# Transposed storage of the inversion's second operands, and a 32-byte pad ahead of the inner activations

## The chip, the cores and the metric

The kernel runs on one core of a Trainium2 chip. The core has five engines that run their own instruction streams and meet through semaphores: TensorE (matmul; its weight loads are shown apart, as PEld), VectorE (DVE), ScalarE (ACT), GpSimd (POOL) and SyncE (SP), which here issues most DMAs. SBUF holds 128 partitions; matmul results go to PSUM. The metric is device microseconds of one execution of the whole program; lower is better.

## The reference, cut to what matters

A two-layer diffusion backbone over 512 latent tokens and 256 context tokens of width 1024. The first layer mixes tokens by windowed attention and by a bidirectional RWKV-7 scan, the second by a Fourier transform; each layer ends in a dense block with a hidden width of 4096. What the change touches is the scan and the dense block:

```python
def step(S, inp):
    r_t, w_t, k_t, v_t, kk_t, a_t = inp
    s_kk = jnp.einsum('bhvk,bhk->bhv', S, kk_t)
    S = (S * w_t[:, :, None, :]
         - s_kk[..., None] * (kk_t * a_t)[:, :, None, :]
         + v_t[..., None] * k_t[:, :, None, :])
    return S, jnp.einsum('bhvk,bhk->bhv', S, r_t)

def channel_mlp(h, w1, w2):
    return jnp.square(jax.nn.relu(h @ w1)) @ w2
```

Everything is float32.

## The kernel before, in words

**The scan, by chunks.** The scan is computed in chunks of 64 steps, two chunks at a time, in six stages `i` (two of context, four of latent tokens), both directions and eight heads together. Inside a chunk the recurrence is a triangular system, so each stage needs the inverses of 32 unit-triangular 64x64 matrices. `prep(i)` and `chunkmats(i)` make the matrices (tiles `ab`), `inverse(i)` replaces their diagonal blocks by inverses, and `chain_step(i, j)` uses them on TensorE. The six inversions come one after another between about 220 and 550 us, woven with the attention and with the projections.

**`inverse(i)`.** The 32x32 diagonal blocks go out through DRAM (tile `Dg`) and come back into tile `Minv` (`M` and its second half `Mb`) with each of the 64 blocks on two of the 128 partitions, one for each of its 16x16 diagonal blocks. VectorE then inverts the 128 of them at once, every partition its own, by block doubling: `R` (tile `Rt`) holds the inverses of the diagonal blocks of size `m`, and for m = 2, 4, 8 two block products give the off-diagonal blocks of size `m`. A product of two m x m blocks has two instructions: `tensor_tensor` (line 820) forms all m*m*m products into `Mt` (`tt`), with the sum's index innermost, and `tensor_reduce` (line 823) sums the innermost index. Step 0 multiplies a block of `M` by a block of `R` into the small tile `pp`, step 1 a block of `R` by `pp` into `R`. For the last doubling, from 16 to 32, the 16x16 products are split over the two halves of the partitions, eight columns each, and made in two halves of eight rows (`r0`): lines 838 (the wide product, 1024 elements per partition) and 840 (its sum), four of each per inversion. There step 0 multiplies by `Yh` (columns 256 to 384 of `Mb`, filled by two ScalarE copies at lines 830 and 831 from the inverse in `R`), and step 1 by `pp`. Further ScalarE copies (832 to 834) lay out other operands, and 843, 844 and 846 put the result in place; then it goes back through DRAM (`D2`, `D3`), and small matmuls (863 to 872) finish the 64x64 inverses in `ab`.

The second operand of every such product is a matrix of which column `j` is multiplied by row `i` of the first, so the sum's index runs down a column. Stored row by row, as `Yh` and `pp` are, a column is read with a stride of a row: 8 elements at line 838 and 820 with m = 8, 4 with m = 4, 2 with m = 2 (32, 16 and 8 bytes). Where step 0 of line 820 reads its column from `R`, the stride is 32 elements.

**The dense blocks.** `mlp(l, ...)` runs twice. Each float32 matrix is split into a rounded part and the rest (`whi`/`wlo`, `hhi`/`hlo`, `zhi`/`zlo`), and `mm3` makes each product from three matmuls (lines 306, 307, 308): weights 128x128 held in the array, 512 columns of activations streamed past. The weights are loaded by DMA into `st`, rounded by ScalarE (line 294) and subtracted by VectorE (line 295). In each of two halves of the hidden width, 16 blocks first stream the normed input `hhi`/`hlo` (the first three blocks of a layer stream `uhi`/`ulo`) and write the squared ReLU as `zhi`/`zlo` (lines 1466 and 1467); then eight output blocks `m` stream the 16 pairs `zhi`/`zlo`. Those are the inner activations. They and the operands of the Fourier layer are taken with `zq` from pool `Q`, 34 slots of 2048 bytes per partition; `hhi`, `uhi` and the weights come from pools `H` and `wp`. For the very last output block, `last()` runs its 512 columns as two parts of 256.

**Order and addresses.** Each engine runs its instructions in the order in which the scheduler put them, and the same holds for DMA issues on SP. Tile addresses come from the pools, in the order of their first use; a pool's tiles begin behind each other. As built, the start addresses per partition are these:

| tiles | first byte, modulo 2048 | modulo 64 |
|---|---|---|
| `whi`, `wlo`, `hhi`, `hlo`, `uhi`, `ulo`, `mhi`, `rwhi`, `d2hi` | 96 | 32 |
| `zhi`, `zlo`, `cshi`, `abhi`, `u1hi`, `u2`, `fwhi` (pool `Q`) | 320 | 0 |

The tiles of `Q` lie from byte 147,776 to 217,408, those of the first row start below byte 101,000.

Of the kernel before, what the change touches and what calls it, by code (L numbers as in the profile page):

```python
# [5 lines left out]
F32 = mybir.dt.float32  # L6
F32R = mybir.dt.float32r
AF = mybir.ActivationFunctionType
ALU = mybir.AluOpType
# [193 lines left out]
def body(tc, I, out):  # L203
# [4 lines left out]
    act, dve, pool, pe = nc.scalar, nc.vector, nc.gpsimd, nc.tensor  # L208
# [203 lines left out]
    def sub(t, base, dims):  # L412
        a = t[:]
        return bass.AP(tensor=a.tensor, offset=a.offset + base, ap=[a.ap[0]] + dims)
# [7 lines left out]
    for g in range(2):  # L422
# [5 lines left out]
        if g == 0:  # L428
            for k in range(8):
                t = h2("sg", name=f"x{k}")  # L430
# [29 lines left out]
    for m in range(GRP):  # L460
        w = []
# [13 lines left out]
    for k in range(8):  # L475
        t = P0.tile([128, C], F32, name=f"c{k}")
# [298 lines left out]
    def inverse(i, o):  # L775
        phase(f"inv{i}")
        ABf = [o.AB[d].rearrange("p c h e t -> p (c h e) t") for d in range(2)]
        if i in I2:
            M, Mb, tt = h2("E", name="Minv"), h2("E", name="Mb"), sB
        else:  # L780
            Mp, tt = p4((128, 1024), "Minv"), p4((128, 1024), "Mt")
            M, Mb = Mp[:, 0:512], Mp[:, 512:1024]
# [25 lines left out]
        R = Rt  # L808
        dve.tensor_scalar(sub(R, 1, [[66, 8]]), sub(M, 1, [[66, 8]]), -1.0, None, ALU.mult)
        pp = P.tile([128, 128], F32, tag="pp", bufs=1, name="pp")  # L810
        for m in (2, 4, 8):
            n, s = 8 // m, 66 * m
            for step in range(2):

                if step == 0:
                    a, b, sb_, rb_ = (M, m), (R, 33 * m), s, 32
                else:
                    a, b, sb_, rb_ = (R, 0), (pp, 0), m * m, m
                for w in range(n):
                    dve.tensor_tensor(sub(tt, m * m * m * w, [[m * m, m], [m, m], [1, m]]), sub(a[0], a[1] + s * w, [[32, m], [0, m], [1, m]]),  # L820
                                      sub(b[0], b[1] + sb_ * w, [[0, m], [1, m], [rb_, m]]), ALU.mult)
                out_ = sub(pp, 0, [[m * m, n], [m, m], [1, m]]) if step == 0 else sub(R, m, [[s, n], [32, m], [1, m]])
                dve.tensor_reduce(out_, sub(tt, 0, [[m * m * m, n], [m * m, m], [m, m], [1, m]]), AX.X, ALU.add, negate=step == 0)

        lo_, up = slice(0, 64), slice(64, 128)
        Rl = R[:, 0:512].rearrange("p (i t) -> p i t", t=32)
        Yh = Mb[:, 256:384].rearrange("p (i t) -> p i t", t=8)
        Yb = Mb[:, 0:256].rearrange("p (i t) -> p i t", t=16)
        oh = Mb[:, 384:512].rearrange("p (i t) -> p i t", t=8)
        act.copy(Yh[lo_], Rl[up, :, 0:8])  # L830
# [4 lines left out]
        for step in range(2):  # L835
            ma, a0, a1 = (M, 16, 32) if step == 0 else (Mb, 0, 16)
            for r0 in (0, 8):
                dve.tensor_tensor(sub(tt, 0, [[128, 8], [16, 8], [1, 16]]), sub(ma, a0 + a1 * r0, [[a1, 8], [0, 8], [1, 16]]),  # L838
                                  sub(Mb, 256, [[0, 8], [1, 8], [8, 16]]) if step == 0 else sub(pp, 0, [[0, 8], [1, 8], [8, 16]]), ALU.mult)
                dve.tensor_reduce(sub(pp, 8 * r0, [[8, 8], [1, 8]]) if step == 0 else sub(Mb, 384 + 8 * r0, [[8, 8], [1, 8]]),  # L840
                                  sub(tt, 0, [[128, 8], [16, 8], [1, 16]]), AX.X, ALU.add, negate=step == 0)
        R3 = R.rearrange("p (i t) -> p i t", t=32)
        dve.tensor_copy(R3[0:64, 0:16, 16:24], oh[0:64])
# [17 lines left out]
        p = pst("iv", (128, 16, 32))  # L861
# [5 lines left out]
        p = pst("iv", (128, 16, 32))  # L867
# [519 lines left out]
    for m in range(8):  # L1387
        p = outhalf(m, 1, rws)
# [6 lines left out]
    p2 = ExitStack()  # L1395
    Q = p2.enter_context(tc.tile_pool(name="Q", bufs=1, reuse_waits="tile"))
    SQP.append(Q)

    def xt(name):
        return h2("sg", name=name)  # L1400
# [147 lines left out]
    for gp in range(2):  # L1548
        for t in range(4):
            p = pst(("mm", "mm", "mm", "ch", "ch", "iv", "mm", "mm")[4 * gp + t], (128, 2, 256))  # L1550
# [24 lines left out]
    for g in range(4):  # L1575
        pp = pst("mm"), pst("mm")
        for w in range(2):
            o = pp[0][:, 0:258] if w == 0 else pp[1][:, 0:256]
            for t in range(4):
                a = [x_[:, g % 2, 128 * w : 128 * w + 128] for x_ in AB[t, g // 2]]  # L1580
                m = [x_[:, 0:258] if w == 0 else x_[:, 256:512] for x_ in d2[t]]
# [17 lines left out]
    for t in range(4):  # L1599
        hi, lo = ax[:, t, 0, :], ax[:, t, 1, :]  # L1600
        m = [x_[:, 0:258] for x_ in d2[t]]
# [15 lines left out]
    for m in range(8):  # L1617
# [3 lines left out]
        w = fou["ws", m]  # L1621
        pq, pp = pst("mm"), pst("mm")
# [93 lines left out]
```

## Time and profile before

| | us |
|---|---|
| runs (3) | 1505.99, 1507.44, 1516.73 |
| median | 1507.44 |
| the profiled execution, its own time | 1519.14 |
| its span in the profile | 1517.4 |
| mean granted clock of TensorE in it | 0.94 |

The profile is of one execution. A group's row has the line, the engine, the operation, result and operands, the shape and the count, then busy time in us and the mean of one in ns, then the idle time of the engine in front of them and what ended it. The chain of work that ended last is followed back from the last instruction, at each step to what released it or to the instruction before it on its engine. A window's row has the busy time of each engine in that stretch, with the number of its instructions, the clock that TensorE was granted, the share of the DMA engines and their rate.

### The profile page before, as it was taken

Reading aid. Unit: us, or ns where it says so; the run is one execution under the profiler, and the core shown is the slowest. Engines: PE = TensorE matmul, PEld = TensorE weight load, DVE = VectorE, ACT = ScalarE, POOL = GpSimd, SP = SyncE. Lnnn points to the kernel's source line nnn. Section 1 sums busy time; section 2 is a strip of 40 time slices with the busy share of each in tenths; the row PEclk is TensorE's granted clock in tenths of the full one; section 3 lists DMA queues with packets and bytes.
Section 4 is the critical chain, followed back from the end, with each engine's and each line's share of the span. In section 5 each row is a group of like instructions: output and inputs, shape, how many; then the busy total and the mean of one; then the engine's idle time right before and its main releaser. Section 6 shows DMA issues by size and latency. Waiting matters only on the chain.

```text
span 1517.4 us, 23544 instructions
## 1 busy us (share of the span) xinstructions
PE 1400.1 (92%) x8700; PEld 1100.2 (73%) x8700; DVE 894.5 (59%) x1598; ACT 673.1 (44%) x1312; POOL 351.3 (23%) x364
## 2 busy tenths in 40 slices
PE   6889898879789899998999999999998999999997
PEld 2668776657566576577777887787887888888886
DVE  3454778888879743377755555566697432333334
ACT  3466685473452322254642244532354642255322
POOL 0444776251453423404000000000055000000001
PEclk8869998966689999999999999999999999999998
DMA  9347885364363431132555555566122333333322
GB/s 363 113 130 235 279 269 149 115 193 119 104 180 110 126 92 35 49 102 87 153 178 190 177 181 168 169 193 192 53 85 77 99 96 98 90 98 97 97 91 70
DMA packets 166146, 208.73 MB, mean 138 GB/s; under 512 B 45000, under 2 KB 78792, under 8 KB 166032
## 3 DMA queue, kind: packets, MB, share of 16 engines
q1 hardware_dynamic: 164144, 205.30, 44.2%
q10 hardware_dynamic: 1376, 1.90, 0.4%
q8 instruction: 68, 1.11, 0.3%
q14 instruction: 46, 0.38, 0.1%
q0 software_dynamic: 512, 0.03, 0.0%
HBM read 180.15 MB, written 27.00 MB: 137 GB/s over the span
## 4 chain that ended last, share of the span: by engine, by line
PE 60%; DVE 17%; DMA 10%; issue 6%; ACT 4%; POOL 2%; SPq 1%; DVEq 0%; ACTq 0%; POOLq 0%
PE ps L308 15%; PE ps L306 15%; PE ps L307 15%; DMA st<-adaB_in 4%; DVE wlo L295 2%; DVE Mt L838 2%; PE ps L223 2%; DVE Mt L820 1%; PE ps L732 1%; PE ps L1156 1%; DMA ada<-adaB_in 1%; DVE st L391 1%; POOL ada L388 1%; PE ps L441 1%; DMA D<-Mt 1%
## 5 line engine op out<-in xcount | busy, mean ns | idle before, releaser
L294 ACT CAST whi<-st 128x512 fp32r<-128x512 f32 x306 | 188.8, 621 | 405.1 <-PE ps L307 369.1
L295 DVE TENSOR_TENSOR wlo<-st,whi 128x512 fp32r<-128x512 f32 x306 | 225.1, 740 | 173.8 <-ACT whi L294 169.8
L308 PE MATMUL ps<-hhi,wlo 128*128 128x512 f32 x600 | 241.2, 402 | 10.2 <-DVE wlo L295 10.2
L306 PE MATMUL ps<-hhi,whi 128*128 128x512 f32 x600 | 239.3, 400 | 5.3 <-ACT hhi L353 3.0
L307 PE MATMUL ps<-hlo,whi 128*128 128x512 f32 x600 | 237.8, 397 | 0.6 <-DVE hlo L354 0.5
L308 PE MATMUL ps<-zhi,wlo 128*128 128x512 f32 (+1 forms) x528 | 205.7, 390 | 3.8 <-DVE wlo L295 3.8
L306 PE MATMUL ps<-zhi,whi 128*128 128x512 f32 (+1 forms) x528 | 205.4, 389 | 0.0
L307 PE MATMUL ps<-zlo,whi 128*128 128x512 f32 (+1 forms) x528 | 205.1, 389 | 0.0
L308 PEld LDWEIGHTS ps<-hhi,wlo 128*128 128x128 f32 x600 | 114.9, 192 | 42.7 <-DVE wlo L295 19.0
L306 PEld LDWEIGHTS ps<-hhi,whi 128*128 128x128 f32 x600 | 114.9, 192 | 31.2 <-ACT hhi L353 3.8
L307 PEld LDWEIGHTS ps<-hlo,whi 128*128 128x128 f32 x600 | 114.8, 191 | 26.0 <-DVE hlo L354 1.8
L308 PEld LDWEIGHTS ps<-zhi,wlo 128*128 128x128 f32 x528 | 99.1, 188 | 28.6 <-DVE wlo L295 6.3
L307 PEld LDWEIGHTS ps<-zlo,whi 128*128 128x128 f32 x528 | 99.2, 188 | 22.6
L306 PEld LDWEIGHTS ps<-zhi,whi 128*128 128x128 f32 x528 | 99.2, 188 | 22.2
L391 DVE CUSTOM_DVE_ANT_0 st<-st,sB,vec 128x512 f32<-128x512 f32 x56 | 42.3, 755 | 121.8 <-DMA st<-adaB_in 121.8
L1525 POOL TENSOR_TENSOR wa<-st 128x512 f32<-128x512 f32 x8 | 12.0, 1502 | 354.6 <-DMA st<-fw_in 338.8
L388 POOL TENSOR_TENSOR ada<-ada,sB 128x512 f32<-128x512 f32 x48 | 74.4, 1575 | 39.2 <-DMA ada<-adaB_in 18.1
L1673 POOL TENSOR_TENSOR rs<-ms,pw 128x2 f32<-128x2 f32 x2 | 1.4, 704 | 338.9 <-DVE ms L1671 338.9
L223 PE MATMUL ps<-identr 128*128 128x512 f32 x132 | 63.6, 499 | 12.6 <-DVE ed L737 5.3
L1467 DVE TENSOR_TENSOR zlo<-s,zhi 128x512 fp32r<-128x512 f32 x64 | 44.0, 689 | 31.2 <-ACT zhi L1466 31.2
L732 PE MATMUL ps<-pr,gq 64*128 64x128 f32 (+1 forms) x384 | 56.7, 312 | 2.7 <-DVE gq L707 2.6
L732 PEld LDWEIGHTS ps<-pr,gq 64*128 64x128 f32 x384 | 49.1, 214 | 13.9 <-issue 9.8
(446 smaller groups left out, 2757.7 us busy)
## 6 DMA issues: line engine op xcount, KB each, us to landing
st<-w_in SPq DMA_DIRECT2D x256, 256.0 KB, 2.8
st<-adaB_in SPq DMA_DIRECT2D x112, 256.0 KB, 3.4
ada<-adaB_in SPq DMA_DIRECT2D x48, 256.0 KB, 4.5
st<-win_in SPq DMA_DIRECT2D x40, 256.0 KB, 3.7
spl_th<-th SPq DMA_DIRECT2D x16, 384.0 KB, 2.8
pgth<-spl_th SPq DMA_DIRECT2D x24, 256.0 KB, 4.4
st<-adaA_in SPq DMA_DIRECT2D x16, 256.0 KB, 5.4
st<-adaA_in SPq DMA_DIRECT2D x8, 512.0 KB, 7.5
```

What stands on the lines that cost most here:

```text
L223: pe.matmul(bass.AP(tensor=a.tensor, offset=a.offset, ap=[a.ap[0], [1, 512]]), identr, identr.unsqueeze(1).to_broadcast([128, 4, 128]), st ...
L294: act.copy(hi, st)
L295: dve.tensor_tensor(lo, st, hi, ALU.subtract)
L306: pe.matmul(o, whi, x[0], start=first, stop=False)
L307: pe.matmul(o, whi, x[1], start=False, stop=False)
L308: pe.matmul(o, wlo, x[0], start=False, stop=last)
L388: pool.tensor_tensor(st, st, su, ALU.mult)
L391: dve.tensor_tensor_reduce(st, st, su, 1.0, col if u else V(vec, "adb", i), ALU.mult, ALU.add, col)
L441: pe.matmul(pa[q : q + 32, :], sT[:, k, :], mats[k], start=k < 4, stop=k >= 4)
L732: pe.matmul(p[:, hp, :wd], o.GQ[d][c][rows, hp, :], o.PR[d][c][rows, hp, :wd], start=True, stop=True)
L838: dve.tensor_tensor(sub(tt, 0, [[128, 8], [16, 8], [1, 16]]), sub(ma, a0 + a1 * r0, [[a1, 8], [0, 8], [1, 16]]), sub(Mb, 256, [[0, 8], [1, ...
L1467: dve.tensor_tensor(lo, s, hi, ALU.subtract)
```

## The change

Two edits. In the inversion, the second operands `pp` and `Yh` are stored transposed, so that the sum's index is innermost in memory: the reductions at lines 823 and 840 write `pp` with their result's axes swapped, the ScalarE copies at 830 and 831 write `Yh` through a swapped view, and the products at 820 (second step) and 838 read their second operand contiguously. What step 0 of line 820 reads stays as it is in `R`. In the dense part, an unused tile of 32 bytes per partition is taken first from pool `Q`; nothing reads or writes it.

```diff
                 if step == 0:
-                    a, b, sb_, rb_ = (M, m), (R, 33 * m), s, 32
+                    a, b, sb_, rb_, cb_ = (M, m), (R, 33 * m), s, 32, 1
                 else:
-                    a, b, sb_, rb_ = (R, 0), (pp, 0), m * m, m
+                    a, b, sb_, rb_, cb_ = (R, 0), (pp, 0), m * m, 1, m
                 for w in range(n):
                     dve.tensor_tensor(sub(tt, m * m * m * w, [[m * m, m], [m, m], [1, m]]), sub(a[0], a[1] + s * w, [[32, m], [0, m], [1, m]]),
-                                      sub(b[0], b[1] + sb_ * w, [[0, m], [1, m], [rb_, m]]), ALU.mult)
-                out_ = sub(pp, 0, [[m * m, n], [m, m], [1, m]]) if step == 0 else sub(R, m, [[s, n], [32, m], [1, m]])
+                                      sub(b[0], b[1] + sb_ * w, [[0, m], [cb_, m], [rb_, m]]), ALU.mult)
+                out_ = sub(pp, 0, [[m * m, n], [1, m], [m, m]]) if step == 0 else sub(R, m, [[s, n], [32, m], [1, m]])
...
-        Yh = Mb[:, 256:384].rearrange("p (i t) -> p i t", t=8)
+        Yh = Mb[:, 256:384].rearrange("p (t i) -> p i t", t=8)
...
-                                  sub(Mb, 256, [[0, 8], [1, 8], [8, 16]]) if step == 0 else sub(pp, 0, [[0, 8], [1, 8], [8, 16]]), ALU.mult)
-                dve.tensor_reduce(sub(pp, 8 * r0, [[8, 8], [1, 8]]) if step == 0 else sub(Mb, 384 + 8 * r0, [[8, 8], [1, 8]]),
+                                  sub(Mb, 256, [[0, 8], [16, 8], [1, 16]]) if step == 0 else sub(pp, 0, [[0, 8], [16, 8], [1, 16]]), ALU.mult)
+                dve.tensor_reduce(sub(pp, r0, [[1, 8], [16, 8]]) if step == 0 else sub(Mb, 384 + 8 * r0, [[8, 8], [1, 8]]),
...
     SQP.append(Q)
+    Q.tile([128, 8], F32, name="zpad")
```

The instructions of each engine, their order and the semaphores that they wait for are the same in both programs; so are the DMA issues. Shapes and strides differ at the lines named, and every 2048-byte tile of `Q` starts 32 bytes later: at 352 modulo 2048, 32 modulo 64.

## The prediction

> **What bounds the kernel now.** I read the page first: busy shares and the chain that ended last. The kernel is TensorE-heavy, with VectorE second on the chain.
>
> ```profile
> span 1517.4 us, 23544 instructions
> PE 1400.1 (92%) x8700; PEld 1100.2 (73%) x8700; DVE 894.5 (59%) x1598; ACT 673.1 (44%) x1312; POOL 351.3 (23%) x364
> ...
> PE 60%; DVE 17%; DMA 10%; issue 6%; ACT 4%; POOL 2%; SPq 1%; DVEq 0%; ACTq 0%; POOLq 0%
> ```
>
> The change touches two places that are limited by different engines, so I cut the span at them. In the view by windows a row gives the window's length, then each engine's busy time and instruction count, the granted clock and the DMA share. Three windows lie around wide products of single inversions (the third, fifth and sixth), four around the dense products that read the inner activations.
>
> ```profile
> core 0: us, PE busy (x) PEld busy (x) DVE busy (x) ACT busy (x) POOL busy (x), PEclk, DMA share, GB/s
> 345.00:369.00 24.00, 24.00 (x143) 19.35 (x143) 20.43 (x35) 4.64 (x12) 0.98 (x1) 0.50 0.47 134
> 405.00:425.00 20.00, 20.00 (x196) 13.90 (x197) 19.54 (x26) 7.60 (x20) 11.28 (x8) 0.97 0.35 96
> 515.00:531.00 16.00, 15.74 (x123) 7.08 (x122) 15.46 (x11) 6.45 (x15) 13.01 (x9) 1.00 0.16 48
> 794.00:888.00 94.00, 93.93 (x402) 75.50 (x403) 50.89 (x109) 22.21 (x36) 0.00 (x0) 1.00 0.58 187
> 976.00:1073.00 97.00, 93.25 (x398) 73.94 (x397) 60.81 (x117) 32.92 (x56) 2.58 (x2) 1.00 0.58 181
> 1226.00:1322.00 96.00, 96.00 (x414) 77.50 (x414) 30.21 (x45) 25.72 (x42) 0.00 (x0) 1.00 0.31 94
> 1404.00:1496.00 92.00, 92.00 (x420) 75.28 (x419) 33.30 (x49) 32.33 (x53) 0.00 (x0) 1.00 0.27 83
> ```
>
> VectorE is 98% and 97% busy in the windows of the fifth and sixth inversion; in the third (345 to 369) TensorE is full too, at a clock of 0.50. In the four dense windows TensorE is 96% to 100% busy and ACT, VectorE and GpSimd at or under 63%: there one matmul's spacing is the time.
>
> **The change, part by part.** No engine gets an instruction more, less or in another place, and no queue a transfer; the waits are the same. Three things change: strides, the place of results, and the start addresses of the tiles of pool Q.
>
> *Wide products (VectorE).* The inversion multiplies small blocks elementwise and sums. The second operand of line 838, and of line 820 in its second step, was read with a stride of 8, 16 or 32 bytes per element; now it is read element after element. The rows to price that are two lines' own views (shortest, median and longest in ns, first and last start) and the groups of instructions (busy us, mean ns of one):
>
> ```profile
> L838 DVE TENSOR_TENSOR Mt<-Minv x12: 2024/2088/3000, 238.4 to 518.6; 128x1024 f32<-128x1024 f32 x12
> L838 DVE TENSOR_TENSOR Mt<-Minv,pp x12: 1998/2043/2827, 246.5 to 526.5; 128x1024 f32<-128x1024 f32 x12
> ```
>
> ```profile
> L820 DVE TENSOR_TENSOR Mt<-Rt,pp x42: 153/206/1721, 227.8 to 513.1; 128x8 f32<-128x8 f32 x24, 128x64 f32<-128x64 f32 x12, 128x512 f32<-128x512 f32 x6
> ```
>
> ```profile
> L1467 DVE TENSOR_TENSOR zlo<-s,zhi 128x512 fp32r<-128x512 f32 x64 | 44.0, 689 | 31.2 <-ACT zhi L1466 31.2
> ...
> L840 DVE TENSOR_REDUCE pp<-Mt 128x64 f32<-128x1024 f32 x12 | 14.5, 1210 | 0.1
> L820 DVE TENSOR_TENSOR Mt<-Rt,pp 128x512 f32<-128x512 f32 x6 | 7.2, 1200 | 0.0
> ...
> L823 DVE TENSOR_REDUCE pp<-Mt 128x64 f32<-128x512 f32 x6 | 4.1, 683 | 0.1
> L823 DVE TENSOR_REDUCE Rt<-Mt 128x64 f32<-128x512 f32 x6 | 4.1, 681 | 0.1
> ```
>
> A contiguous product of 512 elements takes 0.689 us (L1467), what a reduction over 512 takes (0.683). So I price a contiguous product of 1024 as the reduction over 1024, 1.21 us. Line 838 has medians of 2.088 and 2.043 us: it loses 12 x 0.88 + 12 x 0.83 = 20.5 us. The 512-wide second step of line 820 takes 1.20 us in the mean; without its longest (1.721) it is (7.2 - 1.721) / 5 = 1.10, against 0.689, so 6 x 0.41 = 2.4 us. The narrower steps are fixed cost mostly (fastest 0.153 us for 8 elements) and I give them nothing. Together VectorE loses 22.9 us of busy time. The first operand and the first step of line 820 keep their patterns.
>
> What of it lies on the path? In the chain from 215 to 545 us line 838 has this share (pieces: start, length, what; the first and the last of the long ones, and the two cut ones):
>
> ```profile
> by line: DVE Mt L838 8.8%; issue 7.4%; DVE Mt L820 6.5%; PE ps L732 5.8%; PE ps L223 4.2%; DMA D<-Mt 3.8%; DVE Minv L840 2.5%; DVE pp L840 2.5%; POOL ada L388 2.2%; DVE ab L734 2.2%; DMA Minv<-Dg 2.1%; DVE ed L737 2.1%; DVE Sbd L934 2.0%; P
> ...
> 252.89 1.93 DVE Mt L838
> ...
> 340.67 1.72 DVE Mt L820
> ...
> 471.83 0.76 DVE Mt L838
> ...
> 513.15 1.00 DVE Mt L820
> ...
> 526.62 2.76 DVE Mt L838
> ```
>
> 8.8% of 330 us is 29.0 us: twelve of the 24 products nearly whole (1.9 to 3.0 us each) and pieces of two more. Twelve by 0.85 is 10.2, the pieces 0.4, and two wide second steps of line 820 (340.67, 513.15) 0.8: at most 11.4 us with this chain. It would all be won only if nothing else came late. TensorE is next in line (20.00 of 20.00 us busy in the fifth inversion's window, though a busy PE is a modelled end), then the round trip of the inverse through DRAM (D<-Mt, 3.8%). Two of the three inversion windows above are VectorE's and one is TensorE's, so I take two thirds: 7.6 us. Ends: nothing, if TensorE or those transfers are as late; 22.9, if the freed VectorE time also moves work that the chain passes by.
>
> *The price of storing transposed.* The reductions into pp now write with a stride. They write one result per 8 or 16 inputs, and the reduction into Rt, whose eight results each lie in another row of 128 bytes, takes as long as that into pp (0.681 and 0.683). So nothing. ScalarE's two copies into Yh (lines 830 and 831) now write 16 elements apart:
>
> ```profile
> L831 ACT COPY Minv<-Rt x6: 293/294/295, 238.1 to 514.9; 64x128 f32<-64x128 f32 x6
> ...
> L832 ACT COPY Minv<-Rt x6: 404/405/407, 238.4 to 515.2; 64x256 f32<-64x256 f32 x6
> ...
> L846 ACT COPY Mt<-Rt x6: 1974/2029/2060, 258.0 to 531.3; 64x1024 f32<-64x1024 f32 x6
> ```
>
> Contiguous they cost (405 - 294) / 128 = 0.87 ns an element; L846, whose reads are strided, takes 2.029 us where 1024 contiguous ones would take 1.07, so 0.94 ns more each. If a strided write costs as much, a copy grows by 0.12 us; only that of line 831 stands between two VectorE steps, so 0 to 6 x 0.12 = 0.7 us. I take 0.4.
>
> *The pad.* As the kernel is built, every 512-wide operand that streams through TensorE outside pool Q (hhi, uhi, mhi, rwhi), and each weight tile, starts 32 bytes past a multiple of 64; zhi and zlo start on a multiple of 64. The pad moves all of Q by 32 bytes, so that they start like the rest (and a multiple of 256 from the weights). Here are undisturbed runs of both, first and last of 19 matmuls of the same shape, at the same granted clock of 1.00 (start, duration):
>
> ```profile
> 1250.04 0.40 PE L308 MATMUL ps<-zhi,wlo 128*128 128x512 f32 x1
> ...
> 1254.24 0.40 PE L308 MATMUL ps<-zhi,wlo 128*128 128x512 f32 x1
> ```
>
> ```profile
> 1350.13 0.39 PE L308 MATMUL ps<-hhi,wlo 128*128 128x512 f32 x1
> ...
> 1354.21 0.39 PE L308 MATMUL ps<-hhi,wlo 128*128 128x512 f32 x1
> ```
>
> 4.20 / 18 = 233.3 ns for zhi, 4.08 / 18 = 226.7 for hhi: the same three matmuls per step, with the same weight tiles. Two layers by two halves by 8 by 16 by 3 is 1536 such matmuls; the last 48 are cut to 256 columns, so 1488 x 6.6 ns = 9.8 us if zhi comes to hhi's spacing. It goes straight to the end where TensorE is full. In the second dense window it waits for weights five times (5.9 us in all between 1040 and 1075):
>
> ```profile
> PEld ps L308 <- DVE wlo L295: 5.9, 5, 2.0
> ```
>
> About 20 us there, some 86 matmuls, go at VectorE's pace: 0.6 us less, so 9.2. Fourier and 256-column matmuls I leave at nothing: a weight load, not the stream, may set their pace. Ends: nothing, and 9.8.
>
> [...]
>
> **The sum.** -7.6 + 0.4 - 9.2 = -16.4 us. The profiled execution took 1519.1 us (span 1517.4 and 1.7 around it) and would take 1502.7; it is slower than the median of the runs, 1507.4, from which I forecast 1507.4 - 16.4 = 1491.
>
> **Rivals.**
> *The pad does nothing.* Tiles of Q also lie in the upper part of SBUF (from about 147 KB), those that run at 226.7 ns in the lower; if the place and not the 64-byte phase slows zhi, 32 bytes change nothing. For it: no tile of before has one without the other. Against: start phase is the simpler difference. Time: 1507.4 - 7.2 = 1500. [...]
> *VectorE's gain is hidden.* TensorE, full in the third and fifth inversions' windows, or the transfers stay the last to come: 1507.4 + 0.4 - 9.2 = 1499. Against: the chain takes twelve of these products.
> *Slower.* The new phase could be a worse one. After a stall even hhi has a step like this:
>
> ```profile
> 729.30 0.40 PE L306 MATMUL ps<-hhi,whi 128*128 128x512 f32 x1
> 729.54 0.39 PE L307 MATMUL ps<-hlo,whi 128*128 128x512 f32 x1
> ```
>
> 0.24 us. If zhi settled there, the pad would cost 1488 x 6.7 ns = 10.0 us, and with VectorE's 7.2 the kernel would take 1510. It is slower than before from 233.3 + 7200 / 1488 = 238.1 ns on, and by 1% only from about 248, which no settled row shows. The rows speak against it: hhi settles to 226.7 at the very phase that the pad gives.
>
> **How the numbers follow.** Both parts act: 0.70, 1491, own range 1482 to 1499. Pad does nothing: 0.18, 1500. VectorE's gain hidden: 0.09, 1499. Slower phase: 0.03, 1510. For 8 in 10 the range takes in the first case, its VectorE term between nearly nothing and about twice, and the next two with the spread of the runs: 1480 to 1502. One per cent, about what a measurement of this kernel can tell from no change, ends at 1492.4: inside the first case, and I put 0.52 of its 0.70 below that line; the hidden cases add 0.01. So faster 0.53, same 0.45, slower 0.02 (most of the slower case ends within 1%).
>
> **What would show it.** Line 838 near 1.21 us and the 512-wide second step of line 820 near 0.69; the first step as before; lines 830 and 831 at 0.29 to 0.42; line 838's share of the chain down by four tenths, and the dense blocks start about 7 us earlier. The zhi stream at 226.7 ns, and each dense window shorter by about 2.5 us. The prediction is wrong if zhi stays at 233, if line 838 stays at 2 us (then its first operand, not the second, sets its pace), or if the waits of VectorE or TensorE before 545 us grow by what line 838 loses.

## The result, and the profile after

| | before | changed |
|---|---|---|
| median of the runs beside each other, us | 1511.9 (4 runs, 1505.99 to 1516.73) | 1489.8 (4 runs, 1488.17 to 1491.43) |
| ratio, 95% interval | | 0.984 (0.9809 to 0.9872) |
| profiled execution, us | 1519.14 | 1491.43 |
| VectorE busy, us | 894.5 | 871.8 |
| first mhi matmul, after the first matmul, us | 640.6 | 621.2 |
| from the first zhi matmul to the end, us | 720.9 | 712.6 |

The changed kernel is 1.3 to 1.9% faster. The last two rows split it in the profiles: 19.4 us were won before the dense blocks begin, and 8.3 us behind the first zhi matmul. The profiled execution of before was 7 us slower than the median of its runs, so that this split is of 27.7 us, where the medians differ by 22.1. In the experiments below, the medians of transposed_alone and half_transposed each count one run far off the others (1833 and 3217 us), which their ratios leave out.

The page of the changed kernel, busy time and the chain by engine:

```profile
span 1489.7 us, 23544 instructions
...
PE 1380.7 (93%) x8700; PEld 1089.9 (73%) x8700; DVE 871.8 (59%) x1598; ACT 673.8 (45%) x1312; POOL 339.3 (23%) x364
...
PE 63%; DVE 15%; DMA 12%; ACT 4%; issue 4%; POOL 1%; SPq 1%; DVEq 0%; ACTq 0%; POOLq 0%
```

VectorE lost 22.7 us of busy time, and its share of the chain fell from 17% to 15%. The views of the changed lines (shortest, median, longest in ns), and the group of the 512-wide second step (busy us, mean ns):

```profile
L838 DVE TENSOR_TENSOR Mt<-Minv x12: 1206/1225/2066, 239.0 to 495.2; 128x1024 f32<-128x1024 f32 x12
L838 DVE TENSOR_TENSOR Mt<-Minv,pp x12: 1205/1215/1867, 244.6 to 502.9; 128x1024 f32<-128x1024 f32 x12
...
L830 ACT COPY Minv<-Rt x6: 411/412/416, 233.8 to 488.0; 64x128 f32<-64x128 f32 x6
L831 ACT COPY Minv<-Rt x6: 400/408/417, 238.6 to 492.2; 64x128 f32<-64x128 f32 x6
```

```profile
L820 DVE TENSOR_TENSOR Mt<-Rt,pp 128x512 f32<-128x512 f32 x6 | 5.9, 992 | 0.0
```

```profile
L840 DVE TENSOR_REDUCE pp<-Mt 128x64 f32<-128x1024 f32 x12 | 14.6, 1213 | 0.1
```

The products of line 838 went from 2.09 and 2.04 us to 1.22. The sums, whose results are now stored with a stride, still take 1.21, and the two ScalarE copies went from 0.296 and 0.294 to about 0.41. In the view of the chain from 215 to 545 us:

```profile
by line: DVE Mt L820 8.1%; PE ps L223 5.5%; issue 5.1%; PE ps L732 4.2%; DVE Mt L838 3.7%; DMA D<-Mt 2.9%; PE ps L897 2.5%; DMA pgth<-spl_th 2.4%; DMA ada<-adaB_in 2.0%; POOL ada L388 1.7%; ACT Mt L846 1.6%; PE ps L901 1.6%; DMA pgkk<-spl_k
```

Line 838 holds 3.7% of the 330 us, 12.2 us, where it held 29.0. That fall of 16.8 is not time won: the chain also runs through fewer of these products now, and line 820 has gone from 6.5% to 8.1%. What the change is worth has to come from the experiments.

The stream of zhi (start, duration), first and last of 19 matmuls, at a granted clock of 1.00:

```profile
1225.43 0.39 PE L308 MATMUL ps<-zhi,wlo 128*128 128x512 f32 x1
...
1229.51 0.39 PE L308 MATMUL ps<-zhi,wlo 128*128 128x512 f32 x1
```

4.08 / 18 = 226.7 ns, from 233.3. So the products are shorter and the stream is faster, as forecast. What has to be settled is how much each is worth, and why.

Two tables from the traces serve all experiments. The first has the time of each of the six inversions, from the first instruction of line 809 to that of line 843, in us. "Stride kept" means that the products read as before. The last column is the time that TensorE spent at half clock within the third inversion, twice the inversion's length times what its granted clock lacked to 1: in the traces of before and of the changed kernel that clock is always 1.00 or 0.50.

| profile of | 1 | 2 | 3 | 4 | 5 | 6 | sum | third, at half clock |
|---|---|---|---|---|---|---|---|---|
| before | 33.0 | 39.0 | 44.0 | 38.6 | 46.3 | 28.7 | 229.5 | 36.0 |
| before_again (stride kept) | 31.7 | 40.0 | 39.0 | 37.8 | 46.7 | 28.5 | 223.8 | 13.5 |
| pad_alone (stride kept) | 32.9 | 39.8 | 44.7 | 38.9 | 46.3 | 28.5 | 231.1 | 37.0 |
| pad_160 (stride kept) | 31.9 | 39.5 | 38.9 | 38.8 | 46.7 | 28.9 | 224.7 | 22.6 |
| pad_96 (stride kept) | 31.7 | 38.6 | 38.8 | 38.0 | 51.8 | 28.4 | 227.2 | 18.3 |
| weights_phase (stride kept) | 31.7 | 38.8 | 39.1 | 37.2 | 46.8 | 28.7 | 222.2 | 18.7 |
| slow_both (sums strided too) | 34.2 | 40.4 | 42.1 | 42.7 | 48.9 | 31.8 | 240.1 | 23.9 |
| slow_sums | 31.5 | 39.3 | 44.3 | 37.6 | 46.0 | 27.5 | 226.1 | 36.7 |
| half_transposed | 30.3 | 36.4 | 43.9 | 38.0 | 46.9 | 26.8 | 222.3 | 35.9 |
| transposed_alone | 28.1 | 36.0 | 35.4 | 34.4 | 43.2 | 25.9 | 203.0 | 18.0 |
| changed kernel | 29.4 | 36.2 | 35.5 | 34.5 | 43.2 | 25.5 | 204.3 | 18.3 |
| whole_again (changed kernel) | 29.2 | 36.3 | 35.6 | 34.8 | 42.9 | 24.0 | 202.8 | 18.4 |
| ada_behind (transposed) | 29.4 | 35.7 | 35.3 | 34.4 | 43.3 | 25.5 | 203.6 | 17.9 |
| ada_first (transposed) | 29.5 | 36.6 | 38.8 | 34.8 | 43.3 | 24.0 | 207.0 | 25.8 |

The second has the four windows of the zhi matmuls, two in each layer, first to last start, in us.

| profile of | layer 0, first | layer 0, second | layer 1, first | layer 1, second |
|---|---|---|---|---|
| before | 89.5 | 97.9 | 89.4 | 91.0 |
| before_again | 89.7 | 97.2 | 89.4 | 91.0 |
| transposed_alone (no pad) | 89.5 | 97.6 | 89.4 | 91.0 |
| half_transposed (no pad) | 90.1 | 98.2 | 89.4 | 91.0 |
| slow_sums (no pad) | 89.6 | 95.6 | 89.4 | 91.0 |
| slow_both (no pad) | 90.2 | 96.1 | 89.4 | 91.0 |
| pad_alone | 89.2 | 95.6 | 86.8 | 88.9 |
| changed kernel | 88.9 | 96.5 | 86.8 | 88.9 |
| whole_again | 89.9 | 98.4 | 86.8 | 88.9 |
| weights_phase | 88.3 | 97.1 | 86.8 | 88.9 |
| pad_96 | 88.7 | 95.6 | 87.7 | 89.3 |
| pad_160 | 89.4 | 97.6 | 89.4 | 91.0 |
| ada_behind | 88.8 | 100.5 | 86.8 | 88.9 |
| ada_first | 86.8 | 89.1 | 86.8 | 88.9 |

### The profile page after: what moved, and what is told of

It is laid out like the page before. It is cut to its first block, busy times and chain, and to the rows that moved or that the text cites. A ratio compares the mean times of both kernels' runs of the same rounds, so it can differ in the third digit from the quotient of the medians.

```text
span 1489.7 us, 23544 instructions
## 1 busy us (share of the span) xinstructions
PE 1380.7 (93%) x8700; PEld 1089.9 (73%) x8700; DVE 871.8 (59%) x1598; ACT 673.8 (45%) x1312; POOL 339.3 (23%) x364
## 3 DMA queue, kind: packets, MB, share of 16 engines
q1 hardware_dynamic: 164144, 205.30, 44.7%
## 4 chain that ended last, share of the span: by engine, by line
PE 63%; DVE 15%; DMA 12%; ACT 4%; issue 4%; POOL 1%; SPq 1%; DVEq 0%; ACTq 0%; POOLq 0%
PE ps L308 16%; PE ps L307 15%; PE ps L306 15%; DMA st<-adaB_in 6%; DVE wlo L295 3%; PE ps L223 2%; DVE Mt L820 2%; PE ps L1156 1%; PE ps L732 1%; DVE st L391 1%; DMA pgth<-spl_th 1%; PE ps L441 1%; DVE Mt L838 1%; DMA st<-adaA_in 1%; DMA D<-Mt 1%
## 5 line engine op out<-in xcount | busy, mean ns | idle before, releaser
L306 PE MATMUL ps<-zhi,whi 128*128 128x512 f32 (+1 forms) x528 | 202.4, 383 | 0.0
L307 PE MATMUL ps<-zlo,whi 128*128 128x512 f32 (+1 forms) x528 | 202.1, 383 | 0.0
L308 PEld LDWEIGHTS ps<-hhi,wlo 128*128 128x128 f32 x600 | 114.8, 191 | 41.2 <-DVE wlo L295 17.6
L306 PEld LDWEIGHTS ps<-hhi,whi 128*128 128x128 f32 x600 | 114.7, 191 | 31.5 <-ACT hhi L353 3.8
L308 PEld LDWEIGHTS ps<-zhi,wlo 128*128 128x128 f32 x528 | 99.1, 188 | 28.7 <-DVE wlo L295 9.7
L388 POOL TENSOR_TENSOR ada<-ada,sB 128x512 f32<-128x512 f32 x48 | 70.7, 1494 | 40.9 <-DMA ada<-adaB_in 35.0
L732 PEld LDWEIGHTS ps<-pr,gq 64*128 64x128 f32 x384 | 45.1, 198 | 13.2 <-issue 9.7
L732 PE MATMUL ps<-pr,gq 64*128 64x128 f32 (+1 forms) x384 | 52.2, 295 | 2.7 <-DVE gq L707 2.7
```

Source lines behind the costliest of these rows:

```text
L306: pe.matmul(o, whi, x[0], start=first, stop=False)
L307: pe.matmul(o, whi, x[1], start=False, stop=False)
L308: pe.matmul(o, wlo, x[0], start=False, stop=last)
L388: pool.tensor_tensor(st, st, su, ALU.mult)
L732: pe.matmul(p[:, hp, :wd], o.GQ[d][c][rows, hp, :], o.PR[d][c][rows, hp, :wd], start=True, stop=True)
```

## The experiments

### Each part alone, and the spread of the two kernels

**pad_alone**: the kernel before with the pad.

```diff
     SQP.append(Q)
+    Q.tile([128, 8], F32, name="zpad")
```

> The pad without the transposed storage. If the start phase of the zhi and zlo tiles sets the spacing, their matmuls come to about 226.7 ns from 233.3 and the run is 7 to 9 us faster than before, all of it behind the scan; line 838 stays at 2.0 us. Rival (the upper part of SBUF is slow, or the gain in the changed kernel's zhi stages came from something else): spacing stays at 233.3 and the time within 2 us of before.

Measured: 1512.3 us, ratio 0.998 (0.9953 to 1.0007). The 7 to 9 us expected did not come: 3.0 us less, with an interval from 7.1 less to 1.1 more, so that it may be nothing. The trace shows more:

```profile
1250.41 0.39 PE L308 MATMUL ps<-zhi,wlo 128*128 128x512 f32 x1
...
1254.49 0.39 PE L308 MATMUL ps<-zhi,wlo 128*128 128x512 f32 x1
```

The stream of zhi runs at 4.08 / 18 = 226.7 ns, and layer 1's windows are 2.6 and 2.1 us shorter. From the first zhi matmul to the end it takes 713.6 us instead of 720.9; the other profiles at 233.3 ns take 716.8 to 720.6.

**transposed_alone**: the kernel before with all of the diff but the pad.

> The transposed storage without the pad. Line 838 at 1.21 us, zhi spacing 233.3 ns. Theory (only VectorE time on the chain counts, as forecast): 7 to 11 us faster than before. Rival (as the pair of profiles reads, 20 us gone before the dense blocks, because TensorE also spends less time at half clock in the scan): 13 to 20 us faster. With the pad's part added, the two parts should give the whole: about 22 us.

Measured: 1499.9 us, ratio 0.9901 (0.9862 to 0.9939): 15 us less (9 to 21). All six inversions shrink against before_again, from 223.8 to 203.0 us in sum, and the first mhi matmul comes 19.4 us earlier than in the profile of before. That is more than the 7 to 11 us of the theory; what the rival gave as the reason, less time at half clock, is taken up below.

**before_again**: the kernel before, unchanged, treated as an experiment, to see what its own spread does to profiles and times.

> The kernel before, unchanged, for a second profile. Before ran at 1506 to 1507 us twice and at 1516 to 1517 twice. If its time hangs on how long TensorE is granted half clock in the scan (about 106 us of it from 215 to 545 us in the first profile, 75 in the changed kernel's), a faster run of it shows less than 106 us there and the same durations at line 838; if the clock has nothing to do with it, the half-clock time is the same whatever the run's time.

Measured: 1512.2 us, ratio 0.9996 (0.9969 to 1.0023). The time is the same; the profile is not. Its window around the third inversion, from 345 to 369 us:

```profile
core 0: us, PE busy (x) PEld busy (x) DVE busy (x) ACT busy (x) POOL busy (x), PEclk, DMA share, GB/s
345.00:369.00 24.00, 22.14 (x208) 17.30 (x205) 23.97 (x45) 8.53 (x23) 1.14 (x4) 1.00 0.50 139
```

The prediction read the same window of before as TensorE's: 24.00 of 24.00 us busy, with a granted clock of 0.50. Here the clock is 1.00, TensorE does 208 matmuls instead of 143, and VectorE is 23.97 us busy. The third inversion takes 39.0 us instead of 44.0. From 215 to 545 us the half clock takes 82 us in sum, 106 in before, and this execution took 3 us less than the profiled one of before. All fourteen profiles have a stretch of half clock just ahead, with a mean clock of 0.51 to 0.65 from 315 to 345 us (0.60 in before and the changed kernel, 0.65 in before_again); what comes in some executions of a program and not in others is that another follows, to about 369 us. While it lasts it makes TensorE look like the limit.

**whole_again**: the changed kernel once more.

> The changed kernel again, both parts, beside the runs of this call. If the two parts add, it is 20 to 23 us faster than before (ratio 0.985 to 0.987): 15 from the transposed storage and 6 to 7 from the pad. If the pad's part is lost (as the runs of the pad alone, 0.998, could be read), it equals the transposed storage alone: ratio 0.990.

Measured: 1493.5 us, ratio 0.9876 (0.9844 to 0.9908): 19 us less (14 to 24). The interval holds both the sum of the two parts and the transposed storage alone. Its third inversion's window, and that of the first profile of the changed kernel, lie at clocks of 0.98 and 1.00; the latter's row:

```profile
345.00:369.00 24.00, 21.64 (x234) 16.79 (x232) 22.14 (x48) 11.94 (x27) 7.80 (x14) 1.00 0.64 182
```

### How much of VectorE's time is the kernel's time

Three kernels give VectorE other doses. **half_transposed** stores `pp` transposed, but leaves `Yh` as it was.

```diff
-                                  sub(Mb, 256, [[0, 8], [1, 8], [8, 16]]) if step == 0 else sub(pp, 0, [[0, 8], [1, 8], [8, 16]]), ALU.mult)
-                dve.tensor_reduce(sub(pp, 8 * r0, [[8, 8], [1, 8]]) if step == 0 else sub(Mb, 384 + 8 * r0, [[8, 8], [1, 8]]),
+                                  sub(Mb, 256, [[0, 8], [1, 8], [8, 16]]) if step == 0 else sub(pp, 0, [[0, 8], [16, 8], [1, 16]]), ALU.mult)
+                dve.tensor_reduce(sub(pp, r0, [[1, 8], [16, 8]]) if step == 0 else sub(Mb, 384 + 8 * r0, [[8, 8], [1, 8]]),
```

> Half a dose: only the products of the second steps read a transposed operand (pp); Yh stays as before, no pad. VectorE loses 12 x 0.83 + 6 x 0.4 = 12.4 us of the 22.9. If the time follows VectorE's, 9 to 12 us faster than before (each inversion about 2 us shorter, against 3.5 with the full change); if a threshold or the clock's state decides, either nothing or the full 15.

Measured: 1506.0 us, ratio 0.9945 (0.9913 to 0.9978): 8 us less (3 to 13), where 9 to 12 were expected. VectorE is busy 881.3 us, 13.2 less than before. The inversions did not all shrink by 2 us: the first, second and sixth took 2 to 3 us less than in before, the third, fourth and fifth 0.6 less to 0.6 more. This profile has the long half clock in the third inversion, with TensorE busy 24.00 of 24.00 us from 345 to 369 us: there, what VectorE saved was not won. Why the fourth and the fifth did not shrink I did not find.

**slow_sums** turns the loops instead: the products run with the sum's index outermost, read the second operand and write without a stride, and the sums read with one.

```diff
-                dve.tensor_tensor(sub(tt, 0, [[128, 8], [16, 8], [1, 16]]), sub(ma, a0 + a1 * r0, [[a1, 8], [0, 8], [1, 16]]),
-                                  sub(Mb, 256, [[0, 8], [1, 8], [8, 16]]) if step == 0 else sub(pp, 0, [[0, 8], [1, 8], [8, 16]]), ALU.mult)
+                dve.tensor_tensor(sub(tt, 0, [[64, 16], [8, 8], [1, 8]]), sub(ma, a0 + a1 * r0, [[1, 16], [a1, 8], [0, 8]]),
+                                  sub(Mb, 256, [[8, 16], [0, 8], [1, 8]]) if step == 0 else sub(pp, 0, [[8, 16], [0, 8], [1, 8]]), ALU.mult)
...
-                                  sub(tt, 0, [[128, 8], [16, 8], [1, 16]]), AX.X, ALU.add, negate=step == 0)
+                                  sub(tt, 0, [[8, 8], [1, 8], [64, 16]]), AX.X, ALU.add, negate=step == 0)
```

> Storage as before and no pad, but the wide products run their loops in another order, so that their second operand is read eight in a row, while the sums at line 840 read with a stride of 64 elements: the cost is taken from 24 products and given to 24 sums. If what counts is VectorE's total time in the inversion, and strided reads cost a sum what they cost a product (0.83 us for 1024), the products take about 1.2 us, the sums about 2.0, and the time stays that of before within 4 us, with each inversion as long as before (29 to 46 us from line 809 to line 843). Rival: it is the product itself that others wait for or are blocked by (two SBUF inputs, beside GpSimd's), then it is 10 us or more faster than before with the sums slow.

Its two lines:

```profile
L838 DVE TENSOR_TENSOR Mt<-Minv x12: 1208/1226/2194, 238.9 to 512.8; 128x1024 f32<-128x1024 f32 x12
...
L840 DVE TENSOR_REDUCE pp<-Mt x12: 1883/1930/2016, 240.3 to 515.1; 128x64 f32<-128x1024 f32 x12
```

What the products save, the sums take back: VectorE is busy 894.0 us, as before. The run took 1507.0 us, ratio 0.9954 (0.9921 to 0.9988), so 2 to 12 us less, where a change within 4 us was expected. Where these come from I did not find; its profile has the half clock in the third inversion, as the profile of before has. It was compared with the same runs of before as half_transposed, which gained 8 us: between these two no difference in time is shown.

**slow_both** is the opposite dose: products that read the second operand with the old stride and write with one, and sums that read with one.

```diff
-                dve.tensor_tensor(sub(tt, 0, [[128, 8], [16, 8], [1, 16]]), sub(ma, a0 + a1 * r0, [[a1, 8], [0, 8], [1, 16]]),
+                dve.tensor_tensor(sub(tt, 0, [[8, 8], [1, 8], [64, 16]]), sub(ma, a0 + a1 * r0, [[a1, 8], [0, 8], [1, 16]]),
...
-                                  sub(tt, 0, [[128, 8], [16, 8], [1, 16]]), AX.X, ALU.add, negate=step == 0)
+                                  sub(tt, 0, [[8, 8], [1, 8], [64, 16]]), AX.X, ALU.add, negate=step == 0)
```

> The kernel before, with the intermediate tile Mt of the wide products laid out so that the products write it strided and the sums read it strided; the second operands stay as they were. The sums go from 1.21 to 1.93 us (as slow_sums showed), 24 of them, +17 us of VectorE; the products read and write strided and should stay near 2.04 us (if a strided write adds to it, VectorE gains more). Theory, VectorE's own time sets the end of every inversion: each of the six grows by 2.5 to 3 us, and the run by 15 to 17 us against the kernel before (ratio 1.010 to 1.011). Rival, the gain of the transposition came mostly through TensorE's half-clock time in some runs: VectorE's added time costs at most the two thirds of the prediction, 11 us or less, and the inversions grow unevenly, the third not at all where TensorE is full in it.

```profile
L838 DVE TENSOR_TENSOR Mt<-Minv x12: 2020/2102/3167, 240.2 to 523.4; 128x1024 f32<-128x1024 f32 x12
...
L840 DVE TENSOR_REDUCE pp<-Mt x12: 1855/1942/1976, 242.5 to 525.7; 128x64 f32<-128x1024 f32 x12
```

Measured: 1526.4 us, ratio 1.009 (1.0059 to 1.0121), 13.7 us more (8.9 to 18.3). VectorE is busy 913.7 us, 19.2 more. The inversions take 240.1 us in sum, 13 to 18 more than the four profiles of before's storage whose third inversion took 39 us (222.2 to 227.2); each grows, by 0.4 to 4.9 us against before_again. Against before itself the third is shorter, 42.1 us for 44.0, because that profile has the long half clock there. The time is a little under the 15 to 17 us of the first theory, whose range the interval holds; it also holds the rival's 11, so the time does not decide between them.

Put together, the time moved per us of VectorE's busy time by 15 / 23.6 = 0.64 (transposed_alone, 870.9 us busy; 0.4 to 0.9 by its interval) and 13.7 / 19.2 = 0.71 (slow_both, the other way; 0.5 to 1.0), where the prediction had 7.6 / 22.9 = 0.33. half_transposed gives 8.3 / 13.2 = 0.63, but with an interval from 0.25 to 1.0, and beside slow_sums it decides nothing.

Inside the inversions it is more, and here the rival, that the gain came through the clock, can be tested: the table has profiles of both storages with as much half clock in the third inversion. The whole third inversion of weights_phase, which keeps the stride:

```profile
329.80:368.90 39.10, 35.26 (x334) 27.77 (x335) 38.73 (x79) 17.70 (x42) 8.34 (x15) 0.76 0.35 105
```

Of the changed kernel:

```profile
323.90:359.40 35.50, 32.56 (x319) 25.95 (x320) 34.99 (x79) 16.62 (x39) 8.23 (x14) 0.74 0.36 106
```

And of before:

```profile
329.40:373.40 44.00, 41.16 (x319) 33.16 (x320) 38.19 (x80) 17.39 (x40) 9.70 (x14) 0.59 0.36 102
```

At a granted clock of 0.76 and 0.74 VectorE is 99% busy in both, with 79 instructions, and the inversion goes from 39.1 to 35.5 us. In before the clock is 0.59, VectorE is 87% busy and the inversion takes 44.0. The other profiles agree: with 18 to 19 us of half clock it takes 38.8 and 39.1 us with the stride, 35.3 to 35.6 without. So the shorter products are worth 3 to 4 us in that inversion at the same clock, and the long half clock adds about 5 us on top.

### The place of the streamed operand

**weights_phase** moves the weights' tiles and those of the hhi stream instead of zhi alone: 32 bytes ahead of each.

```diff
+    wp.tile([128, 8], F32, name="wpad")
...
+    H.tile([128, 8], F32, name="hpad")
```

As that program is built, zhi then lies a multiple of 256 bytes from the weights, but at a multiple of 64, and hhi 32 bytes past a multiple of 256 from them.

> No pad in Q. Instead 32 bytes ahead of the weight tiles and 32 more ahead of pool H: the weights whi and wlo now start on a multiple of 64 like zhi and zlo, hhi still 32 past one. If what counts is that the streamed operand and the weights have the same phase, zhi comes to 226.7 ns and hhi goes to about 233. If it is the streamed operand's own phase, zhi stays at 233 and hhi at 226.7 whatever the weights.

In the timeline of TensorE, first and last of 19 matmuls of each kind (line 309 is 308 of the others):

```profile
1250.03 0.39 PE L309 MATMUL ps<-zhi,wlo 128*128 128x512 f32 x1
...
1254.11 0.39 PE L309 MATMUL ps<-zhi,wlo 128*128 128x512 f32 x1
...
1350.25 0.39 PE L309 MATMUL ps<-hhi,wlo 128*128 128x512 f32 x1
...
1354.45 0.40 PE L309 MATMUL ps<-hhi,wlo 128*128 128x512 f32 x1
```

The two have changed places: zhi at 4.08 / 18 = 226.7 ns, hhi at 4.20 / 18 = 233.3. So a start on a multiple of 64 does not slow zhi, nor does its place in the upper part of SBUF; the paces follow the distance between streamed operand and weights. Layer 1's windows take 86.8 and 88.9 us, as with the pad. The single run took 1512.0 us.

**pad_96** and **pad_160** make the pad 96 and 160 bytes, so that zhi lies 64 and 128 bytes past a multiple of 256 from the weights.

```diff
+    Q.tile([128, 24], F32, name="zpad")
```

```diff
+    Q.tile([128, 40], F32, name="zpad")
```

> The pad is 96 bytes, nothing else changed: zhi starts 32 past a multiple of 64 as with 32 bytes, but 64 and no longer 0 from the weights modulo 256. If the phase modulo 64 decides, zhi runs at 226.7 ns; if modulo 128 or 256, it stays at 231 to 235.

> The kernel before with a pad of 160 bytes instead of 32, so that zhi lies 128 bytes modulo 256 from the weights (32 bytes put it at 0, 96 bytes at 64). If the distance counts modulo 128, zhi's matmuls stand 226.7 ns apart as with the 32-byte pad and the second layer's windows take 86.8 and 88.9 us; if it counts modulo 256 or more, they stand at 229 to 233 ns and these windows take 87.7 to 91 us. In both cases the run's time lies within what the kernel before scatters over.

First and last of 19, of pad_96 and then of pad_160:

```profile
1250.37 0.39 PE L308 MATMUL ps<-zhi,wlo 128*128 128x512 f32 x1
...
1254.49 0.39 PE L308 MATMUL ps<-zhi,wlo 128*128 128x512 f32 x1
```

```profile
1250.18 0.39 PE L308 MATMUL ps<-zhi,wlo 128*128 128x512 f32 x1
...
1254.38 0.39 PE L308 MATMUL ps<-zhi,wlo 128*128 128x512 f32 x1
```

4.12 / 18 = 228.9 ns and 4.20 / 18 = 233.3. So a multiple of 64 is not enough, nor one of 128, and the 228.9 is neither of the two paces expected of pad_96. A stream's own start does not explain it: 160 bytes past a multiple of 256 gave 228.9 (zhi in pad_96) and 233.3 (hhi in weights_phase). Of the distances tried modulo 256, 0 gives 226.7 ns, 64 gives 228.9, and 32, 128 and 224 (the kernel before) give 233.3. The runs took 1511.6 and 1518.0 us, within the scatter of before.

### Why the pad gains less in layer 0

Layer 1's windows shrink by 2.6 and 2.1 us in every profile with the 32-byte pad, as 384 and 336 matmuls by 6.6 ns would have it. Layer 0's first shrinks by 0.6 in the changed kernel and not at all in whole_again. The sum of layer 0's two windows is 185.2 to 188.3 us in the seven profiles at 233.3 ns, and 184.8, 185.4 and 188.3 in pad_alone, the changed kernel and whole_again: no gain is clear of that spread. The waits of TensorE's weight loads between 777 and 866 us of the changed kernel, which is that window (total us, times, longest):

```profile
PEld ps L308 <- DVE wlo L295: 2.8, 6, 0.8
```

In before the same window, from 796 to 886 us, had one:

```profile
PEld ps L308 <- DVE wlo L295: 0.4, 1, 0.4
```

In whole_again, which gained nothing there, such waits come to 3.9 us in the first window and 9.1 in the second (6.8 in the changed kernel, 5.9 in before). In layer 0, VectorE also carries the 56 background pieces of adaB (line 391), which stand ahead of the split of the weights on its queue.

**ada_behind** issues each piece behind the load and split of a block's weights instead of ahead of them, in both loops of layer 0.

```diff
                 for kh in range(2):
-                    if l == 0:
-                        ada_bg(24 + (32 * half + 13 + 2 * m + kh) * 56 // 60)
                     w = split_w(load(I["w2"][l, half, m, kh]))
+                    if l == 0:
+                        ada_bg(24 + (32 * half + 13 + 2 * m + kh) * 56 // 60)
```

> The changed kernel, with the pieces of adaB's product in layer 0 issued behind the load and the split of the dense weights instead of ahead of them. Theory: in layer 0 the pad's gain is lost because wlo's subtraction stands on VectorE behind a reduction that waits for its DMA; with the order turned round TensorE waits less for wlo, layer 0's two windows of zhi matmuls shrink by 2 us each as layer 1's did, and its windows of hhi matmuls by some us too: 5 to 12 us faster than the changed kernel, 1478 to 1485. Rival, the weights come late because of their own DMA and not of the reduction: no change, 1490; or the reductions, pushed back, delay the chain that needs adaB: slower than 1490.

Measured: 1499.7 us, ratio 0.991 (0.9874 to 0.9946): not faster than the changed kernel, where 1478 to 1485 were expected. The first window stays at 88.8, the second grows to 100.5, and the loop over f between them from 92.1 to 97.5 us. A piece moved behind one split stands ahead of the next one; that this is why is my reading.

**ada_first** takes the pieces out of the loops over m altogether and issues all of them in the loops over f.

```diff
-                    ada_bg(24 + max(0, 32 * half + f - 3) * 56 // 60)
+                    ada_bg(24 + 28 * half + (f + 1) * 28 // 16)
...
-                    if l == 0:
-                        ada_bg(24 + (32 * half + 13 + 2 * m + kh) * 56 // 60)
```

> The changed kernel, with the 56 background pieces of adaB of layer 0 issued in the loops over f alone (28 in each half) and none in the loops over m, so that VectorE has no reduction that waits for adaB's DMA while the zhi matmuls run. Theory, the reductions ahead of wlo take the pad's gain in layer 0: layer 0's two windows of zhi matmuls become as short as layer 1's, 86.8 us for the first (88.9 in the changed kernel) and about 94 for the second (96.5), TensorE's waits for wlo go out of them, and come back, or grow, in the loops over f. Rival, the weights of layer 0 come late by their own: both windows stay at 88.9 and 96.5. The run as a whole: between 1485 and 1500, since the loops over f now hold 28 pieces instead of 14 to 15 each.

The windows of layer 0 (zhi, the loop over f, zhi), first of ada_first, then of the changed kernel:

```profile
802.00:889.00 87.00, 87.00 (x386) 72.03 (x385) 32.14 (x53) 21.74 (x35) 0.00 (x0) 1.00 0.37 114
889.00:992.00 103.00, 93.43 (x386) 71.98 (x385) 66.26 (x149) 44.94 (x77) 0.00 (x0) 0.98 0.68 210
992.00:1081.00 89.00, 89.00 (x394) 73.72 (x394) 40.09 (x58) 32.68 (x54) 3.13 (x2) 1.00 0.36 109
```

```profile
777.00:866.00 89.00, 88.37 (x386) 71.51 (x385) 47.76 (x103) 21.69 (x35) 0.00 (x0) 1.00 0.56 182
866.00:958.00 92.00, 90.09 (x386) 71.41 (x385) 50.04 (x106) 46.19 (x77) 0.00 (x0) 1.00 0.56 178
958.00:1055.00 97.00, 92.71 (x404) 74.92 (x404) 59.04 (x115) 32.02 (x54) 2.58 (x2) 1.00 0.56 177
```

Without adaB the zhi windows are full of TensorE work: 87.00 of 87.00 and 89.00 of 89.00 us. They take 86.8 and 89.1 us instead of 88.9 and 96.5, as layer 1's do (86.8 and 88.9); the second is 5 us shorter than expected. Layer 1's windows differ by 2.6 and 2.1 us with and without the pad, so I take its full gain to be in these too; this order was not run without the pad. The price is in the loops over f. In the one between them, TensorE's weight loads wait:

```profile
PEld ps L308 <- DVE wlo L295: 16.1, 16, 2.2
```

It takes 103.2 us instead of 92.1, and the first zhi matmul comes 25 us later than in the changed kernel. In sum the run takes 1515.4 us, where 1485 to 1500 were expected, ratio 1.0006 (0.9973 to 1.0038) against the kernel before. So adaB's pieces in the zhi windows of layer 0 make TensorE wait for weights there, which takes the pad's gain, but neither of these two orders wins it for the whole kernel.

## Why the prediction was right in the whole, and wrong in its parts

**VectorE's busy time: right.** 22.9 us less forecast, 22.7 measured. Line 838 came out at 1.22 us for 1.21; the 512-wide second step of line 820 only at (5.9 - 1.774) / 5 = 0.83 us without its longest, for 0.69, so that it lost 1.6 us instead of 2.4.

**What of it lies on the path: too small by half, and this is the step that failed.** "Two of the three inversion windows above are VectorE's and one is TensorE's, so I take two thirds: 7.6 us." The runs gave 15 (9 to 21). In the profiles the first mhi matmul comes 615.5 to 622.2 us after the first matmul with the transposed storage (five profiles), and 634.3 to 642.7 in the seven in which VectorE is as busy as before (slow_sums is one).

Two things were wrong in that step. The window that looked TensorE's was a stretch of half clock that before_again does not have; with the clock at 1.00 VectorE was busy 23.97 of 24.00 us there, and that inversion shrank by 3.5 us like the others. The reading fits an execution with that stretch: the third inversion of half_transposed, which has it, did not shrink. What was wrong was to take it for the kernel. And the 11.4 us were no upper bound: the chain names one engine at each moment, and ten of the 24 products were off it in that one profile, yet all six inversions shrank, by 2.3 to 3.8 us each against before_again, 19.5 in sum. That the products off the chain count because VectorE's instructions run in order, and what stands behind them is late too, is my reading; the runs show the size only.

That the gain came through the clock instead is not borne out. before_again and the changed kernel have nearly the same mean clock from 215 to 545 us, 0.88 and 0.89, and third inversions with the same half clock differ by 3 to 4 us, as shown above. The long half clock adds some 5 us to the third inversion: 44.0 to 44.7 us in before, pad_alone and slow_sums, for 38.8 to 39.1 in the four others that keep the stride. None of the five profiles of the full transposed storage has it at that length; in ada_first, with 25.8 us of half clock, the third inversion takes 38.8. Whether the change makes it rarer, and so wins some of its time that way as well, is open: I did not try to force it or to prevent it.

**ScalarE's copies: right.** 0.12 us each forecast, 0.116 and 0.114 measured. Their 0.4 us on the path cannot be told from the rest.

**The pad: right in what a matmul gains, mis-sized in the term for stalls.** 6.6 ns per matmul came true, though not by the phase modulo 64: pad_96 has the same phase and runs at 228.9 ns. Layer 1 gave 4.7 us, which is 720 matmuls by 6.6 ns. Layer 0 was to give its 5.1 less 0.6 for waiting weights; its two windows gave 2.0 us in the changed kernel, 2.6 in pad_alone and 0.9 the other way in whole_again. So 4 to 7 us instead of 9.2. The 0.6 counted the waits that before showed; with the faster stream there were more of them (2.8 and 3.9 us for 0.4 in the first window, 6.8 and 9.1 for 5.9 in the second), since the splits of the weights, behind adaB's pieces, did not become faster: in the first window line 295 took 0.687 us in before and 0.686 in the changed kernel (medians of 33), and VectorE waited 38.9 and 41.2 us for adaB's transfers. The Fourier matmuls were left at nothing: from the last zhi matmul of layer 0 to the first of layer 1, the stretch that holds them, it takes 158.4 us before and 158.2 after.

**The sum.** -16.4 forecast; the ratio of the first runs is worth 19 to 29 us, that of whole_again 14 to 24. The time came within 1.2 us of the forecast because the forecast started from 1507.4, the median of three runs, where the kernel before has 1512 to 1516 with more of them. The transposition's term was too small by about 8 and the pad's too large by 2 to 5. That these misses cancel is luck.

**The rivals.** "The pad does nothing" falls with weights_phase: the place in SBUF is not what slows zhi, which runs at 226.7 ns there. "VectorE's gain is hidden" falls with transposed_alone; only in the third inversion of half_transposed, within the long half clock, was it so. "Slower" did not come; but the hhi stream was slowed by as much in weights_phase, to 233.3 ns at a distance of 32.

## What to carry to other kernels

An engine that is 97% busy in a window and one that looks full at half clock are not two votes: look at the granted clock first, and take a second profile of the same program before a window is given to an engine (from 345 to 369 us the clock was 0.50 in before and 1.00 in before_again). The chain that ended last gave no upper bound for what a shorter operation is worth: 11.4 us by the chain, 15 (9 to 21) in the runs of transposed_alone, 19.5 gone from the changed kernel's inversions against before_again. VectorE was 93% to 98% busy in five of the six inversions of before and 87% in the third; most of its saving was won inside them (19.5 of 22.7 us), and about two thirds in the whole run (0.64 and 0.71). And a faster stream is worth its price only as long as what feeds it keeps up (in the first zhi window of layer 0 the waits for weights grew from 0.4 us to 2.8 and 3.9): price the stalls that will be new, and not only those that the profile shows.

## What the runs showed of the hardware

- The pace of the 512-column matmuls of the dense blocks followed the distance, modulo 256 bytes, between the streamed operand and the weights in SBUF: 226.7 ns at 0, 228.9 at 64, 233.3 at 32, 128 and 224. No other distance was tried, and why it counts no run shows.
- A product of 1024 float32 elements took 1.22 us with contiguous operands, 2.04 to 2.09 with the second operand read at a stride of 32 bytes, and hardly more (2.06 to 2.10) when the result was strided too; a sum over 1024 took 1.21 contiguous and 1.91 to 1.94 with a stride of 256 bytes. These strides cost 0.68 to 0.86 ns per element; shorter ones were met only in the narrow steps of line 820, and what they cost there was not measured apart.
- At the same place of the program, from 345 to 369 us, TensorE was granted a mean clock of 0.50 to 0.57 in four profiles (before, pad_alone, slow_sums, half_transposed), 0.79 in two (pad_160, slow_both), and 0.89 to 1.00 in the other eight. The two profiles of one program, before and before_again, had 0.50 and 1.00 and took 1519.1 and 1516.1 us.
